# The first block's adaLN scale on TensorE, with the v weights' loads cut and reordered

## The chip, the cores and the metric

The kernel runs on one core of a Trainium2 chip. The metric is the device time of one execution in microseconds (us); lower is better. Before the change the median of three runs is 1084.25 us (1083.64 to 1084.68).

The core has five engines that run side by side, each with its own list of instructions taken in order: TensorE (PE in the profile; its weight loads are listed as PEld), VectorE (DVE), ScalarE (ACT), GpSimd (POOL) and SyncE (SP). Here SyncE only issues DMAs; GpSimd issues some as well. SBUF and PSUM have 128 partitions; TensorE writes its results to PSUM.

## The reference, cut to what matters

Two layers, each of a token mixer and a SwiGLU network, on x of 512 tokens by 1024 channels in float32. Every sub-layer normalizes its input and then shifts and scales it by vectors that come from a conditioning vector c (adaLN). The part that the change touches is the very first one:

```python
def ada_modulation(c, w, b):
    m = jax.nn.silu(c) @ w + b
    shift, scale, gate = jnp.split(m, 3, axis=-1)
    return shift[:, None, :], scale[:, None, :], gate[:, None, :]

shift, scale, gate = ada_modulation(c, mix_ada_w[0], mix_ada_b[0])
h = rms_norm(x, mix_pre_g[0]) * (1.0 + scale) + shift
qkv = (h @ w_qkv).reshape(B, S, 3, SB_HEADS, SB_HEAD_DIM)
```

After it come stick-breaking attention, its output projection, the network, a token-mixing layer and a second network. They are not touched.

## The kernel before, in words

Matrix products are made from float32 operands that are split in two: a high part, which ScalarE rounds to the matmul's format, and a low part, the difference, which VectorE makes. Three products of high and low parts (high by high, high by low, low by high) are added up in PSUM. The 1024 channels are eight blocks of 128, called k = 0 to 7, with the channels of a block on the partitions.

**The start** (lines 324 to 347). SP's queue issues, in this order: `pack` (c, the identity, the pre-norm's gain), the four token tiles of x, the adaLN weights `ra[0]` of block 0, the first and second v weights (`raw`: 256 rows by 512 columns each, the first for the left half of v's columns and the second for the right), `ra[1]`, `ra[2]`, the third v weights (`rawv`), `ra[3]`, the fourth v weights (`rawv`). Each adaLN block is one tile of 128 partitions by 2 by 1026: for each channel of the block (on the partition) the 1024 weights of its scale, then its bias and a one, and the same for its shift. The remaining blocks `ra[4]` to `ra[7]`, and the v weights from the fifth on, are issued later, when a buffer comes free (four for `ra`, two for `raw`).

**Normalizing and turning.** ScalarE takes silu(c) as `sc`, and TensorE spreads it over all partitions with eight matmuls (line 736). The sums of squares of the four token tiles are taken on VectorE (one) and ScalarE (three); `norm0` scales a tile by its reciprocal root on VectorE, and `turn0(tt, q)` turns four of its eight blocks on TensorE into a PSUM bank. `turned0(tt, q, act)` copies such a bank to `xhT` in two pieces of 128 by 256 on ScalarE. `idle0` issues transposes whose results nobody reads.

**The adaLN sums.** `ada_row(k, i)` (line 710) multiplies a block's 1026 numbers by the spread silu(c) on VectorE and adds them up along the row in the same instruction; i = 0 gives 1 + scale, i = 1 the shift. For k = 0, ScalarE then multiplies the scale by the gain (line 787).

**The first step, k = 0** (lines 767 to 807). ScalarE rounds the first row block of the first v weights (`first_high`), makes the high part of block 0's h (`hTh`) in two halves of 256 tokens, and VectorE makes the low part of the weights (`first_low`), h itself in place, and its low part (`low0`). TensorE begins the v products, with four banks per half of v's columns.

**The loop over k = 1 to 7** (line 814). Per k TensorE has 24 matmuls: two halves of the columns, four token tiles, three products. On VectorE stand the two `ada_row` sums of block k + 1 with the low part of block k between them; on ScalarE the high part of block k + 1 (`high0`). The weights of the next two blocks are rounded in the odd steps, and loads are issued there too: `ra[4]` to `ra[7]` in steps 1 to 4, and one or two later v weights.

From line 344 to line 838 the order on TensorE, VectorE and ScalarE is the order in which the code is written (`pe["chain"]`, `dve.chain`, `act.chain`): each instruction is put behind the one before it on its engine. GpSimd and SP have no such chain; the framework places their instructions. PSUM has six banks that are handed round under the tag `b` and two under the tag `p`; a new use of a bank waits for the last reader of the old one.

The v products are followed by those of q and k (`pqk` in the profile), which are mixed with the attention.

Of the kernel before, what the change touches and what calls it, by code (L numbers as in the profile page):

```python
# [8 lines left out]
F32 = mybir.dt.float32  # L9
F32R = mybir.dt.float32r  # L10
AF = mybir.ActivationFunctionType
ALU = mybir.AluOpType

P = 128
T = 512
NT = T // P
D = 1024
KD = D // P
# [7 lines left out]
def trunk(ctx: ExitStack, tc: tile.TileContext, A: dict, out: bass.AP):  # L26
    nc = tc.nc

    consts = ctx.enter_context(tc.tile_pool(name="consts", bufs=1))
    wraw = ctx.enter_context(tc.tile_pool(name="wraw", bufs=2))  # L30
# [3 lines left out]
    small = ctx.enter_context(tc.tile_pool(name="small", bufs=4))  # L34
# [9 lines left out]
    def nm(s):  # L44
        uid[0] += 1
        return f"{s}_{uid[0]}"
# [5 lines left out]
    def bank(name, tag="b"):  # L52
        return psum.tile([P, 512], F32, tag=tag, bufs=6 if tag == "b" else 2, name=nm(name))
# [22 lines left out]
    dve, act = Written(nc.vector), Written(nc.scalar)  # L76
# [22 lines left out]
    def transpose(o, i):  # L99
        last_tp[0] = nc.tensor.transpose(o, i, ident)  # L100
        pe_op(last_tp[0])
# [6 lines left out]
    def load(dst, src, queue=nc.sync):  # L108
        return queue.dma_start(out=dst, in_=src)
# [8 lines left out]
    stream = []  # L118
# [5 lines left out]
    raws = []  # L124

    def wload():

        src, a, b, key = stream[len(raws)]
        if src is None:
            raws.append(block_loads(key[1]))  # L130
            return
        raw = wraw.tile([P, a, b], F32, tag="raw", name=nm("raw"))
        b = load(raw[:], src)
        if key == ("wout", 1):
            ready[2] = b
        raws.append(raw)
# [31 lines left out]
    def block_loads(idx):  # L168

        x = wraw.tile([P, KD, P], F32, tag="raw", name=nm("rawx"))
        y = fwork["raw"].tile([P, KD, P], F32, tag="raw2", name=nm("rawy"))
        load(x[:], A["wx"][idx])
        b = load(y[:], A["wy"][idx])
        if idx == (1, 0):
            order(b, ready[2])
        return x, y
# [138 lines left out]
    def ada0_raw(k):  # L318

        raw = stp.tile([P, 2, D + 2], F32, tag="ra", bufs=4, name=nm("ada0"))  # L320
        load(raw[:], A["ada0w"][k])
        return raw

    pack = consts.tile([P, KD + P + 2 * KD], F32, name="pack")
# [2 lines left out]
    cols = pack[:, KD + P :].rearrange("p (a b) -> p a b", a=2)  # L327
    x0 = [slot(F32, "x0", 1, 1024)[:, 0, :] for _ in range(NT)]
    for tt, xt in enumerate(x0):
        load(xt, A["x"][tt * P : (tt + 1) * P, :])  # L330
    ra = {0: ada0_raw(0)}
    wload()
    wload()
    ra[1] = ada0_raw(1)
    ra[2] = ada0_raw(2)
    for n in (2, 3):
        raws.append(stp.tile([P, 2, 512], F32, name=f"rawv{n}"))
        load(raws[n][:], stream[n][0])
        if n == 2:
            ra[3] = ada0_raw(3)  # L340
    ones_r = consts.tile([P, P], F32R, name="ones")[:]
    scr = stp.tile([P, D + 2], F32, name="scr")
    nc.gpsimd.memset(scr[:, D:], 1.0)
# [3 lines left out]
    sc = consts.tile([P, KD], F32, name="sc")  # L347
# [115 lines left out]
    def hTk(hT, k, lo, n):  # L463
        h, l = hT[k // 2]
        return h[:, k % 2, lo : lo + n], l[:, k % 2, lo : lo + n]
# [198 lines left out]
    def norm0(tt, sd, r1):  # L664
        dve.reciprocal(r1[:], sd[:])
        dve.tensor_scalar(x0[tt], x0[tt], r1[:, 0:1], None, ALU.mult)
# [3 lines left out]
    def turn0(tt, q):  # L670
        ps = bank("tp0", "p" if q and tt > 1 else "b")
        for k in range(4):
            kk = q * 4 + k
            transpose(ps[:, k * P : (k + 1) * P], x0[tt][:, kk * P : (kk + 1) * P])
        tps[tt, q] = ps

    def turned0(tt, q, engine):
        ps = tps[tt, q]
        for k2 in range(2):
            dst = xhT[q * 2 + k2][:, :, tt * P : (tt + 1) * P]  # L680
            src = ps[:, k2 * 256 : (k2 + 1) * 256].rearrange("p (a b) -> p a b", a=2)
            if engine is dve:
                dve.tensor_copy(dst, src)
            else:
                act.activation(dst, src, AF.Copy)
# [24 lines left out]
    def ada_row(k, i):  # L710

        if i == 0:
            ab[k] = small.tile([P, 2], F32, tag="ab", name=nm("ab"))
        w = ra[k][:, i, :]
        dve.scalar_tensor_tensor(
            w, w, 1.0, scr[:], ALU.mult, ALU.mult, accum_out=ab[k][:, i : i + 1]
        )
        if i == 1 and k:
            dve.tensor_scalar(ab[k][:, 0:1], ab[k][:, 0:1], cols[:, 0, k : k + 1], None, ALU.mult)

    ab = {}
# [20 lines left out]
    def idle0(n, into=warm):  # L742
        for i in range(n):
            transpose(into[:, i % 4 * P : (i % 4 + 1) * P], ident)
# [15 lines left out]
        turn0(tt, 1)  # L760
    norm0(2, *r0[2])
    turn0(2, 0)
    turn0(2, 1)
    norm0(3, *r0[3])
    turn0(3, 0)
    turn0(3, 1)
    vb = [[bank("v0") for _ in range(2)], [bank("v1")]]
    idle0(20, vb[0][0])
    ada_row(0, 0)
    ada_row(0, 1)  # L770
    ws = [wtile(2, 512, WIDE) for _ in range(2)]
    got.extend(ws)
# [2 lines left out]
    def first_high(hf, k):  # L775
        act.activation(ws[hf][0][:, k, :], raws[hf][:, k, :], AF.Copy)

    def first_low(hf, k):
        h, l = [t[:, k, :] for t in ws[hf]]
        dve.tensor_tensor(l, raws[hf][:, k, :], h.bitcast(F32), ALU.subtract)  # L780

    for tt in range(NT):
        if tt == NT - 1:
            turned0(0, 1, act)
        turned0(tt, 0, act)
    scale, shift = [ab[0][:, i : i + 1] for i in range(2)]
    act.activation(scale, scale, AF.Copy, scale=cols[:, 0, 0:1])
    first_high(0, 0)
    x00, (h00, l00) = xhT[0][:, 0, :], hTk(hT, 0, 0, T)
    for c in (slice(0, 256), slice(256, T)):  # L790
        act.activation(h00[:, c], x00[:, c], AF.Identity, scale=scale, bias=shift)
    first_low(0, 0)
    dve.tensor_scalar(x00, x00, scale, shift, ALU.mult, ALU.add)
    first_high(1, 0)
    for tt in (2, 3, 1):
        turned0(tt, 1, act)
    vb[1] += [bank("v1", "p") for _ in range(2)] + [bank("v1")]
    vb[0] += [bank("v0") for _ in range(2)]
# [800 lines left out]
def _layout(i):  # L1599

    f = np.ascontiguousarray

    def fout(w):
        m = w.shape[1] // P
        return w.reshape(KD, P, m, P).transpose(2, 1, 0, 3)

    def blocks(a, b):

        return (
            np.concatenate([a[:, :, :4], b[:, :, 4:]], 2),  # L1610
            np.concatenate([a[:, :, 4:], b[:, :, :4]], 2),
        )

    def slabs(w):
        return w.reshape(-1, P, 1, w.shape[1])

    def vhalf(w):

        return w.reshape(4, 2, P, 2, 512).transpose(3, 0, 2, 1, 4)

    a = {}

    a["x"] = i["x"][0][::-1]
    wqkv = i["sb_w_qkv"][0]
    a["wqk"] = np.stack([fout(wqkv[:, :D]), fout(wqkv[:, D : 2 * D])], 1)
    a["wv"] = vhalf(wqkv[:, 2 * D :])
    a["wo"] = slabs(i["sb_w_o"][0])
    gu = [(fout(i["ffn_w_gate"][l]), fout(i["ffn_w_up"][l])) for l in range(2)]
    a["wgu"] = np.stack([np.stack([g[:3], u[:3]], 1) for g, u in gu])
    a["wx"], a["wy"] = [np.stack(t) for t in zip(*[blocks(g[3:], u[3:]) for g, u in gu])]  # L1630
    a["wdown"] = np.stack([slabs(i["ffn_w_down"][l]) for l in range(2)])
    a["win_u"] = fout(i["tm_w_in"][0][:, :D])
    a["win_v"] = vhalf(i["tm_w_in"][0][:, D:])
    a["wout"] = slabs(i["tm_w_out"][0])
    a["ws"] = i["tm_w_s"][0][:, ::-1, ::-1].transpose(2, 0, 1)
    a["bs"] = i["tm_b_s"][0][:, ::-1].reshape(1, D)
    ada, adab = [], []
    for l in range(2):
        for n in ("mix", "ffn"):
            w, b = i[n + "_ada_w"][l], i[n + "_ada_b"][l]  # L1640
            ada.append(w.reshape(KD, P, 3, D).transpose(2, 0, 1, 3))
            adab.append(b.reshape(3, 1, D))
    a["ada"], a["adab"] = np.stack(ada), np.stack(adab)
    w = i["mix_ada_w"][0].reshape(KD, P, 3, KD, P)
    b0 = i["mix_ada_b"][0]
    t = np.zeros((KD, P, 2, D + 2), np.float32)
    for n in range(2):
        part = w[:, :, 1 - n].reshape(D, KD, P)
        t[:, :, n, :D] = part.transpose(1, 2, 0)
        t[:, :, n, D] = b0[(1 - n) * D : (2 - n) * D].reshape(KD, P)  # L1650
    t[:, :, 0, D + 1] = 1.0
    a["ada0w"] = t
    a["pre_g"] = np.stack([i["mix_pre_g"][0], i["ffn_pre_g"][0], i["mix_pre_g"][1], i["ffn_pre_g"][1]])
    a["post_g"] = np.stack(
        [i["mix_post_g"][0], i["ffn_post_g"][0], i["mix_post_g"][1], i["ffn_post_g"][1]]
    )
    r = np.arange(P)
    one = np.ones((P, P), np.float32)
    cols = [
        i["mix_pre_g"][0].reshape(KD, P).T, i["tm_ln_g"][0].reshape(KD, P).T,  # L1660
    ]
    a["pack"] = np.concatenate([i["c"][0].reshape(KD, P).T, np.eye(P, dtype=np.float32), *cols], 1)
    a["consts"] = np.stack([np.where(r[:, None] >= r[None, :], one, 0 * one), one], 1)
    return {k: f(v) for k, v in a.items()}
# [17 lines left out]
```

## Time and profile before

| what | value |
|---|---|
| median of three runs | 1084.25 us |
| the profiled execution | 1085.17 us |
| its span, first to last instruction | 1083.4 us |
| TensorE's mean granted clock | 0.998 |
| TensorE, VectorE, ScalarE, GpSimd busy | 1070.5, 906.5, 592.1, 40.4 us |
| bytes moved by DMA, mean rate | 176.09 MB, 163 GB/s |

How to read it. Times in the rows of a timeline are microseconds from the span's start, then the duration; a row such as `L92 MATMUL v<-wh,hTh ... x4` merges four neighbours of one kind, and its duration reaches from the first one's start to the last one's end. In `out<-in` stand the names of tiles: `ada` and `ra` are the adaLN blocks (the loads are named `ada`), `raw` and `rawv` the v weights as loaded, `wh` and `wl` their high and low parts, `hTh` and `hTl` those of h, `tp` and `xhT` the turned input, `ab` the scale and shift, `sc` silu(c). Brackets at the end of a row give the engine's idle time just before and what ended it. A matmul's end is modelled, and neighbours overlap, so one that is listed with 0.39 us may follow the one before it after 0.23. Line 66 is the helper through which all of VectorE's and ScalarE's instructions of the listing go, line 92 that of the matmuls, line 100 that of the transposes and line 109 that of the loads.

### The profile page before, as it was taken

The numbers are of one execution on the slowest core, as the hardware profiler recorded it, in microseconds if no ns is written. First come the engines' busy times: TensorE is split into PE (matmuls) and PEld (weight loads), VectorE is DVE, ScalarE is ACT, GpSimd is POOL, SyncE is SP. The second block draws the span as 40 slices with busy tenths as digits, with TensorE's granted clock in tenths as the row PEclk, the third lists the DMA queues.
The fourth block names the chain that finished last, engine by engine and source line by source line (L and its number), as shares of the span: only waits on it lengthen the run. The fifth ranks groups of instructions, "written<-read, shape, count | busy, mean of one in ns | idle before, by whom it ended". The sixth has DMA issues, their size and how long they took to land.

```text
span 1083.4 us, 18162 instructions
## 1 busy us (share of the span) xinstructions
PE 1070.5 (99%) x7348; PEld 974.2 (90%) x7348; DVE 906.5 (84%) x1159; ACT 592.1 (55%) x976; POOL 40.4 (4%) x71
## 2 busy tenths in 40 slices
PE   8999999999999999999999999999999999999997
PEld 7888878779999999988887988988999999989896
DVE  6859889759999999987678865759999999879986
ACT  7656767747555555562144535537555555565552
POOL 1021111000000000010000000001000000000000
PEclk9999999999999999999999999999999999999999
DMA  9686454453244454358884585333245443223433
GB/s 363 231 253 176 142 150 156 156 195 137 79 122 171 137 156 136 101 183 286 272 269 174 196 271 173 101 135 126 90 137 175 134 142 129 85 78 99 134 101 154
DMA packets 51154, 176.09 MB, mean 163 GB/s; under 512 B 5627, under 2 KB 6139, under 8 KB 50046
## 3 DMA queue, kind: packets, MB, share of 16 engines
q1 hardware_dynamic: 45022, 153.95, 43.1%
q0 software_dynamic: 6048, 20.98, 6.0%
q8 instruction: 57, 0.93, 0.3%
q14 instruction: 27, 0.22, 0.1%
HBM read 164.43 MB, written 8.39 MB: 160 GB/s over the span
## 4 chain that ended last, share of the span: by engine, by line
PE 83%; DMA 8%; DVE 5%; ACT 2%; issue 1%; SPq 0%; DVEq 0%; ACTq 0%
PE r L92 31%; PE y L92 9%; PE pqk L92 8%; PE X L92 8%; PE v L92 7%; PE gu L92 6%; DMA rawada<-in_ada 4%; PE u L92 4%; PE M L92 3%; PE z L92 2%; DMA rawv<-in_wv 2%; PE av L92 1%; PE tw L100 1%; DMA raw<-in_wdown 1%; DVE wl L66 1%
## 5 line engine op out<-in xcount | busy, mean ns | idle before, releaser
L66 ACT ACTIVATE wh<-raw 128x1024 fp32r<-128x1024 f32 (+1 forms) x112 | 116.6, 1047 | 133.2 <-DMA raw<-in_wdown 52.2
L66 DVE TENSOR_TENSOR wl<-raw,wh 128x1024 fp32r<-128x1024 f32 (+1 forms) x112 | 133.7, 1201 | 51.8 <-ACT wh L66 51.2
L92 PE MATMUL r<-Sh,wh 128*128 128x256 f32 x608 | 167.9, 276 | 0.3 <-ACT e L66 0.3
L92 PE MATMUL r<-Sh,wl 128*128 128x256 f32 x608 | 167.9, 276 | 0.0
L92 PE MATMUL r<-Sl,wh 128*128 128x256 f32 x608 | 167.8, 276 | 0.0
L92 PE MATMUL y<-wh,as 128*128 128x512 f32 x480 | 150.7, 391 | 1.0 <-DVE G L66 1.0
L66 ACT ACTIVATE e<-r 128x256 f32<-128x256 f32 x114 | 43.0, 378 | 133.2 <-PE r L92 133.1
L92 PEld LDWEIGHTS r<-Sh,wh 128*128 128x128 f32 x608 | 114.1, 188 | 0.6 <-ACT e L66 0.5
L92 PEld LDWEIGHTS r<-Sl,wh 128*128 128x128 f32 x608 | 114.1, 188 | 0.1
L92 PEld LDWEIGHTS r<-Sh,wl 128*128 128x128 f32 x608 | 114.1, 188 | 0.0
L92 PEld LDWEIGHTS y<-wh,as 128*128 128x128 f32 x480 | 90.1, 188 | 20.1 <-DVE G L66 1.7
L92 PE MATMUL y<-wl,as 128*128 128x512 f32 x240 | 93.7, 390 | 0.0
L66 DVE TENSOR_TENSOR wl<-f,wh 128x1024 fp32r<-128x1024 f32 x76 | 92.6, 1219 | 0.0
L92 PE MATMUL r<-hTh,wh 128*128 128x256 f32 x304 | 84.0, 276 | 0.0
L92 PE MATMUL r<-hTh,wl 128*128 128x256 f32 x304 | 83.9, 276 | 0.0
L92 PE MATMUL r<-hTl,wh 128*128 128x256 f32 x304 | 83.9, 276 | 0.0
L66 ACT ACTIVATE wh<-f 128x1024 fp32r<-128x1024 f32 x76 | 80.5, 1059 | 5.9 <-DVE f L66 4.7
L92 PE MATMUL X<-wh,as 128*128 128x512 f32 (+1 forms) x240 | 64.8, 346 | 0.0
L92 PE MATMUL r<-hTh,b 128*128 128x256 f32 x304 | 57.9, 276 | 0.0
L92 PEld LDWEIGHTS r<-hTh,wh 128*128 128x128 f32 x304 | 57.1, 188 | 0.4 <-DVE gu L66 0.2
L92 PEld LDWEIGHTS r<-hTl,wh 128*128 128x128 f32 x304 | 57.1, 188 | 0.0
L92 PEld LDWEIGHTS r<-hTh,wl 128*128 128x128 f32 x304 | 57.1, 188 | 0.0
(236 smaller groups left out, 2826.7 us busy)
## 6 DMA issues: line engine op xcount, KB each, us to landing
rawada<-in_ada SPq DMA_DIRECT2D x56, 512.0 KB, 5.0
raw<-in_wdown SPq DMA_DIRECT2D x44, 512.0 KB, 4.4
rawy<-in_wy SPq DMA_DIRECT2D x38, 512.0 KB, 3.6
rawx<-in_wx SPq DMA_DIRECT2D x38, 512.0 KB, 4.0
rawada<-in_ada POOLq DMA_DIRECT2D x24, 512.0 KB, 4.1
ada<-in_ada0w SPq DMA_DIRECT2D x8, 1026.0 KB, 11.2
raw<-in_wqk SPq DMA_DIRECT2D x16, 512.0 KB, 4.0
raw<-in_wgu SPq DMA_DIRECT2D x12, 512.0 KB, 3.6
```

The costliest lines, as they stand in the source:

```text
L66: b = f(*a, **k)
L92: b = nc.tensor.matmul(o, l, r, start=start, stop=stop, skip_group_check=True)
L100: last_tp[0] = nc.tensor.transpose(o, i, ident)
```

## The change

- **Layout.** For block 0 the scale's weights are stored with the summed index on the partitions: partition p holds, for each of the eight blocks of c, the 128 weights that go from channel p of that block of c to the 128 channels of block 0. Bias and one stay where they were.
- **The sum.** Instead of `ada_row(0, 0)` on VectorE, eight TensorE matmuls of plain float32, with those weights as the loaded operand and one column of silu(c) as the moving one, add up the 128 scales in one PSUM column (`sps`). They stand between the first turn of token tile 2 and that of tile 3. The second turn of tile 2 now follows the first of tile 3. GpSimd makes `base` = (bias + 1) times the gain, and ScalarE makes the scale as gain times sum plus `base`.
- **Idle transposes.** 20 become 2.
- **ScalarE and VectorE at k = 0.** Seven pieces are copied ahead of the scale instead of ten; the last piece of tile 3 follows the high part of h, and the first tile's second half joins the other three later. The first half of the high part of h moves to VectorE.
- **Loads.** `ra[0]` comes in two loads, scale and shift. The first and second v weights come in halves of 128 rows: the first halves of both, `ra[1]`, the second halves, `ra[2]`; then the third and the fourth v weights, then `ra[3]`.

```diff
     def ada0_raw(k):
 
         raw = stp.tile([P, 2, D + 2], F32, tag="ra", bufs=4, name=nm("ada0"))
-        load(raw[:], A["ada0w"][k])
+        for c in (slice(0, 1), slice(1, 2)) if k == 0 else (slice(0, 2),):
+            load(raw[:, c, :], A["ada0w"][k][:, c, :])
         return raw
...
     ra = {0: ada0_raw(0)}
-    wload()
-    wload()
-    ra[1] = ada0_raw(1)
-    ra[2] = ada0_raw(2)
+    raws.extend(wraw.tile([P, 2, 512], F32, tag="raw", name=nm("raw")) for _ in range(2))
+    for k in range(2):
+        for n in range(2):
+            load(raws[n][:, k, :], stream[n][0][:, k, :])
+        ra[k + 1] = ada0_raw(k + 1)
     for n in (2, 3):
         raws.append(stp.tile([P, 2, 512], F32, name=f"rawv{n}"))
         load(raws[n][:], stream[n][0])
-        if n == 2:
-            ra[3] = ada0_raw(3)
+    ra[3] = ada0_raw(3)
...
-    def turned0(tt, q, engine):
+    def turned0(tt, q, engine, k2s=range(2)):
         ps = tps[tt, q]
-        for k2 in range(2):
+        for k2 in k2s:
...
     norm0(2, *r0[2])
     turn0(2, 0)
-    turn0(2, 1)
+    ab[0] = small.tile([P, 2], F32, tag="ab", name=nm("ab"))
+    scale, shift = [ab[0][:, i : i + 1] for i in range(2)]
+    base = small.tile([P, 1], F32, name="base")
+    nc.gpsimd.tensor_scalar(
+        base[:], ra[0][:, 0, D : D + 1], ra[0][:, 0, D + 1 : D + 2], cols[:, 0, 0:1], ALU.add, ALU.mult
+    )
+    sps = bank("scale", "p")[:, 0:1]
+    for k in range(KD):
+        mm(sps, ra[0][:, 0, k * P : (k + 1) * P], sc[:, k : k + 1], k == 0, k == KD - 1)
     norm0(3, *r0[3])
     turn0(3, 0)
+    turn0(2, 1)
     turn0(3, 1)
     vb = [[bank("v0") for _ in range(2)], [bank("v1")]]
-    idle0(20, vb[0][0])
-    ada_row(0, 0)
+    idle0(2, vb[0][0])
     ada_row(0, 1)
...
     for tt in range(NT):
-        if tt == NT - 1:
-            turned0(0, 1, act)
-        turned0(tt, 0, act)
-    scale, shift = [ab[0][:, i : i + 1] for i in range(2)]
-    act.activation(scale, scale, AF.Copy, scale=cols[:, 0, 0:1])
+        turned0(tt, 0, act, range(2 - (tt == NT - 1)))
+    act.activation(scale, sps, AF.Identity, scale=cols[:, 0, 0:1], bias=base[:])
     first_high(0, 0)
     x00, (h00, l00) = xhT[0][:, 0, :], hTk(hT, 0, 0, T)
-    for c in (slice(0, 256), slice(256, T)):
-        act.activation(h00[:, c], x00[:, c], AF.Identity, scale=scale, bias=shift)
+    c = [slice(0, 256), slice(256, T)]
+    dve.tensor_scalar(h00[:, c[0]], x00[:, c[0]], scale, shift, ALU.mult, ALU.add)
+    act.activation(h00[:, c[1]], x00[:, c[1]], AF.Identity, scale=scale, bias=shift)
+    turned0(NT - 1, 0, act, (1,))
     first_low(0, 0)
     dve.tensor_scalar(x00, x00, scale, shift, ALU.mult, ALU.add)
     first_high(1, 0)
-    for tt in (2, 3, 1):
+    for tt in (0, 2, 3, 1):
         turned0(tt, 1, act)
...
         part = w[:, :, 1 - n].reshape(D, KD, P)
         t[:, :, n, :D] = part.transpose(1, 2, 0)
+        if n == 0:
+            t[0, :, n, :D] = part[:, 0].reshape(KD, P, P).transpose(1, 0, 2).reshape(P, D)
         t[:, :, n, D] = b0[(1 - n) * D : (2 - n) * D].reshape(KD, P)
```

## The prediction, made before the result was known

> **What bounds the kernel now.** I read the page first, then the waits of the first 80 us, then the chain that ended last in the same stretch. The page:
>
> ```profile
> span 1083.4 us, 18162 instructions
> ...
> PE 1070.5 (99%) x7348; PEld 974.2 (90%) x7348; DVE 906.5 (84%) x1159; ACT 592.1 (55%) x976; POOL 40.4 (4%) x71
> ```
>
> TensorE is busy in all but 13 us. So an edit near the start is worth exactly what it moves the point from which TensorE never stops again. Where it stops today is in the waits of 0 to 80 us (who waited for what: total, times, longest):
>
> ```profile
> ACT wh L66 <- DMA rawv<-in_wv: 3.3, 1, 3.3
> ...
> ACT wh L66 <- DMA raw<-in_wv: 2.5, 2, 2.0
> ...
> PE v L92 <- ACT hTh L66: 1.1, 1, 1.1
> ```
>
> and the chain says what is behind the 1.1 us (start, length, what):
>
> ```profile
> 9.39 16.51 DMA rawv<-in_wv
> ...
> 25.92 1.06 ACT wh L66
> 26.98 0.71 ACT hTh L66
> ...
> 27.73 32.94 PE v L92 x144
> 60.67 14.28 PE pqk L92 x63
> ```
>
> The fourth v weights land at 25.9; ScalarE, whose order is written out, rounds them before it makes hTh of the third block (k = 2), and TensorE waits for that until 27.73. From there it runs without a gap: 144 matmuls in 32.94 us are 5.49 us for one step of 24. Whatever the change does, the time after is the time before minus what the starts of k = 2, k = 3, k = 4 and so on gain, the smallest gain deciding. The next rows are the timeline of ScalarE, TensorE and the queue at those starts:
>
> ```profile
> 20.85 0.50 PE L92 MATMUL v<-wh,hTh 128*128 128x512 f32 x1
> ...
> 23.96 0.21 DVE L66 TENSOR_SCALAR ab<-ab,pack 128x1 f32<-128x1 f32 x1
> ...
> 24.45 12.00 SPq L109 DMA_DIRECT2D raw<-in_wv  x2
> ...
> 31.30 0.82 ACT L66 ACTIVATE hTh<-xhT,ab 128x512 fp32r<-128x512 f32 x1 [2.77 <-DVE ab L66]
> ...
> 35.94 1.06 ACT L66 ACTIVATE wh<-raw 128x1024 fp32r<-128x1024 f32 x1 [2.02 <-DMA raw<-in_wv]
> 36.91 0.80 ACT L66 ACTIVATE hTh<-xhT,ab 128x512 fp32r<-128x512 f32 x1
> ...
> 38.75 0.39 PE L92 MATMUL v<-wh,hTh 128*128 128x512 f32 x1
> ```
>
> The important one is at 35.94. The sixth v weights (second half of the columns, third pair) were issued at 24.45 and land at 35.94, and hTh of k = 4 stands behind their rounding: it ends at 37.71, and TensorE begins k = 4 at 38.75. So only 1.0 us lies between this second late transfer and TensorE. It costs nothing today because the 1.1 us stall came before it.
>
> **The path to the first v matmul.** The start, in order of time:
>
> ```profile
> 3.06 3.49 PEld L92 LDWEIGHTS sc<-pack,sc 128*128 128x128 f32 x16 [3.06 <-ACT sc L66]
> ...
> 3.08 0.51 SPq L109 DMA_DIRECT2D ada<-in_ada0w  x1
> ...
> 6.42 1.30 PEld L100 LDWEIGHTS warm<-pack 128*128 128x128 f32 x6
> ...
> 10.00 1.51 POOL L396 MEMSET G<- 128x1024 f32 x1
> 10.74 0.86 PEld L100 LDWEIGHTS tp<-pack,x 128*128 128x128 f32 x8 [0.60 <-issue]
> ...
> 10.91 2.83 ACT L66 ACTIVATE xhT<-tp 128x256 f32<-128x256 f32 x10
> ...
> 11.24 0.83 DVE L66 TENSOR_SCALAR x<-x,r 128x1024 f32<-128x1024 f32 x1
> 11.83 0.62 POOL L109 DMA_DIRECT2D G<-in_adab  x1 [0.32 <-POOL G L396]
> 11.99 1.22 DVE L66 SCALAR_TENSOR_TENSOR ada<-ada,scr 128x1026 f32<-128x1026 f32 x1
> ...
> 13.01 2.21 PEld L100 LDWEIGHTS v<-pack 128*128 128x128 f32 x20
> ...
> 13.13 1.22 DVE L66 SCALAR_TENSOR_TENSOR ada<-ada,scr 128x1026 f32<-128x1026 f32 x1
> 13.55 0.37 ACT L66 ACTIVATE ab<-ab,pack 128x1 f32<-128x1 f32 x1
> 13.73 0.71 ACT L66 ACTIVATE wh<-raw 128x512 fp32r<-128x512 f32 x1
> ...
> 14.46 1.09 ACT L66 ACTIVATE hTh<-xhT,ab 128x256 fp32r<-128x256 f32 x2
> 14.47 0.69 DVE L66 TENSOR_TENSOR wl<-raw,wh 128x512 fp32r<-128x512 f32 x1
> ...
> 15.22 1.18 PE L92 MATMUL v<-wh,hTh 128*128 128x512 f32 x4
> ...
> 15.59 0.55 DVE L66 TENSOR_SCALAR xhT<-xhT,ab 128x512 f32<-128x512 f32 x1 [0.42 <-ACT hTh L66]
> ```
>
> Two chains meet at 14.46: ScalarE's ten copies out of PSUM from 10.91, and VectorE's two sums of 1.22 us from 11.99. The change takes three copies (0.28 us each) and one sum off that path, but adds a step on TensorE, which sat in its 20 idle transposes.
>
> *The sum by TensorE.* A matmul of plain f32 is two loads and two multiplications in this trace (16 for the eight of sc), so eight matmuls are 16. Three rows price one: 0.218 us (3.49 / 16) at the start, 0.217 (1.30 / 6) in the warm-up transposes, 0.108 (0.86 / 8) for the transposes just before the new step's place. The moving operand is one column here, so I take the load alone at the nearest row's rate: 16 x 0.108 = 1.73 us. The lower bound is one load per matmul, 0.86; the upper is 3.49. Their weights must be there:
>
> ```profile
> ada<-in_ada0w SPq DMA_DIRECT2D x1, 1026.0 KB, 8.8
> ...
> 6.00:8.00 2.00, 2.00 (x11) 2.00 (x11) 1.18 (x5) 1.83 (x5) 0.00 (x0) 1.00 1.00 397
> ...
> 30.00:32.00 2.00, 2.00 (x11) 1.65 (x10) 2.00 (x4) 0.70 (x1) 0.00 (x0) 1.00 1.03 435
> ...
> 34.00:36.00 2.00, 2.00 (x10) 1.68 (x9) 2.00 (x4) 0.06 (x1) 0.00 (x0) 1.00 0.09 35
> ```
>
> (The last columns of the windows are granted clock, DMA share and GB/s.) The whole block, issued at 3.08, lands at 11.9; its first half, 513 KB at 397 GB/s, 1.3 us sooner, at 10.6. The four transposes ahead of the sum load from 10.74 to 11.17, so nothing waits. The sum takes 11.17 to 12.90; the four transposes of the last token tile, which now stand behind it on TensorE, to 13.33; ScalarE, done with its six other copies by 12.6, copies one piece until about 13.75, makes the scale by 13.95 (0.18 from its start to the next row's), and rounds the weights until 14.65. VectorE has the shift at 13.2 with one sum fewer, does half of hTh meanwhile, then the low part of the weights (0.69), and starts on xhT at 15.3, not 15.59. First v matmul: 14.75 for 15.22.
>
> *What is moved beside it.* The second copy of the last tile now follows hTh and is needed by the fourth v matmul; at 0.28 us it comes about 0.2 us late for it, and is repaid while TensorE would wait for VectorE at k = 1 (it began at 20.85, behind VectorE's two sums). The scale's PSUM buffer is handed on to the last transposes, which therefore wait for the scale at 13.95; they and two idle transposes are 6 x 0.108 = 0.65 us and end by 14.6, before the rounding does. GpSimd's small base step has no row; its neighbours, the memset at 10.00 and the issue that ends at 12.45, are the most it can stand behind, and the scale wants it at 13.75. I cost it at nothing, up to 1.3 us of cover.
>
> So the chain on VectorE that leads to hTh of k = 1 is 0.3 us sooner: k = 1 starts at 20.55. The first row of a step after a wait is 0.11 us longer (0.50 against 0.39), so k = 2 is due at 20.55 + 0.11 + 5.49 = 26.15, k = 3 at 31.64, k = 4 at 37.13.
>
> *The transfers.* The pieces of a load become smaller: one adaLN block from 8.2 KB per partition to 4.1, two v weights from 4 KB to 2. The window of 6 to 8 us, in which x moves in 4 KB pieces, shows 397 GB/s at full share, that of 30 to 32, with adaLN blocks in 8.2 KB pieces, 435 / 1.03 = 422, so halving costs 6%: 0.16 us on a block of 2.6 us, and by the same ratio 0.17 on the two weights. All that follows in the queue lands 0.33 us later for the same bytes ahead of it. The fourth weights have one block fewer ahead: 25.9 - 2.6 + 0.3 = 23.6; rounded by 24.7, hTh of k = 2 (ready from 23.96 + 0.21) ends at 25.5, before 26.15. That stall goes. The fourth adaLN block lands where those weights did, 26.2; today hTh of k = 3 begins 4.3 us after the rounding ends at 26.98, so it would begin near 29.3 and end at 30.1, before 31.64. No new stall there.
>
> *What is late next.* The sixth weights. SP's queue carries the same bytes up to them, from the same start, so they land at 35.94 + 0.33 = 36.27. From there to the end of hTh are 0.97 + 0.80: 38.04. TensorE, due at 37.13, waits for it and starts (0.05 behind it, and with the longer first step of 0.11) as if at 38.20. Against 38.75 that is a gain of 0.55 us of the 1.62 that TensorE was ahead. Later steps have more room: the first q weights' low part,
>
> ```profile
> 57.23 1.23 DVE L66 TENSOR_TENSOR wl<-raw,wh 128x1024 fp32r<-128x1024 f32 x1 [2.32 <-ACT wh L66]
> ```
>
> ends at 58.46 for a use at 60.67, and it depends on transfers and VectorE, not on TensorE. The 0.55 reaches the end. The profiled execution took 1085.17 us, 1.8 more than its span and 0.9 more than the median of the three runs; by it the kernel after would show a span of 1082.85, and by the median 1084.25 - 0.55 = 1083.7.
>
> **Rivals.** *The sixth weights come sooner than their bytes say.* From 34 to 36 us the queue moves 35 GB/s: some engines' remainders. Should the new pieces even these out, the landing falls by up to 2 us, the wait at k = 4 goes, and all 1.62 us stay: 1082.6. Against it: no piece after the fourth adaLN block changes.
>
> *TensorE's clock falls.* Eighteen idle transposes go, and while ScalarE and VectorE work from 12.9 to 14.7, TensorE has ten transposes and some idle time. If it fell back to the rate of its start (0.217 per load for 0.108) for as long as that lasted there, from 3.06 to at least 7.72, half of 4.7 us would be lost: k = 4 due at 37.13 + 2.33 = 39.46, 0.7 slower, 1085.0. It decides from a loss of 1.6 us on. For it speaks that transposes were all that ran before 15.22; against it that the first four v matmuls, after seven microseconds of nothing but transposes, took 1.18 us together, which is the full rate, and that the changed kernel runs real matmuls at 11.2. (The granted clock can't decide it: the window of 6 to 8 us shows 1.00 although the loads in it are 0.217 apart.) The Trainium skill (TensorE: Matmul & The Clock Gate, Part 4: PE-mode transpose) says that transposes do not count as work for the clock; by that rule the v matmuls of the kernel before would have begun at half rate, and the trace disagrees with it.
>
> *The eight small matmuls are slow.* Each adds to the same PSUM column. If each waited for the last, the mean duration of the start's rows would count, not their spacing:
>
> ```profile
> L92 PE MATMUL sc<-pack,sc 128*128 128x128 f32 x16 | 3.8, 431 | 3.1 <-ACT sc L66 3.1
> ```
>
> 16 x 0.431 = 6.9 us is 5.2 more than I took; k = 4 is due at 42.3, 3.5 slower, 1087.8. At 3.49 for all it is due at 38.9: no change. It decides above 3.4 us, and shows beyond 0.2% above 5.5. For it speaks that the eight at the start write to different columns, so that no row shows such a chain of one column; against it the q matmuls of the chain, 24 in a row into one bank, which are 0.227 apart (14.28 / 63) while one v matmul of the same size lasts 0.39 (the row at 38.75).
>
> *The stall at k = 2 stays*, because the fourth adaLN block or VectorE takes the weights' place: then only the 0.3 us of the start are left, at most, 1084.0 to 1084.3.
>
> **How the numbers follow.** Forecast 0.60; sixth weights sooner 0.15; clock 0.08; slow small matmuls 0.10; stall stays 0.07. The bounds of the small sum alone do not move the forecast: at 0.86 us TensorE only waits longer at k = 4, at 2.8 it is just in time. The range takes the forecast, the sixth weights sooner, the stall, and the milder half of the rest: 1082.5 to 1085.1. What a measurement of this kernel can tell from no change is about 0.2%, 2.2 us. Faster by that needs the sixth weights sooner and a small sum at its lower bound: 0.04. Slower by that needs the slow sum above 5.5 us, or a disturbed order later: 0.06. Within it: 0.90.
>
> **What would show it.** Right: eight matmuls into the scale in about 1.7 us from 11.2; first v matmul near 14.75; no idle time ahead of k = 2; a new idle stretch of about 0.8 us ahead of k = 4, behind hTh, behind a rounding that waits for the sixth weights near 36.3; TensorE's unbroken run from 38.1. Wrong: those weights landing before 35.4 or after 36.8, a sum over 3.4 us, TensorE's loads spaced by 0.2 us after 12, or any wait at k = 2 or k = 3.

## The result: 10.8 us slower, by matmuls that the change does not touch

The changed kernel takes 1094.74 us (median of five runs, 1094.38 to 1095.26) against 1083.97 (1083.64 to 1084.68): a ratio of 1.010, 95% interval 1.0085 to 1.0114. The forecast was 1083.7, the range 1082.5 to 1085.1. The profiled execution took 1095.22 us.

The page after, with two of the costliest groups (the last columns: busy us, mean ns of one, idle time before):

```profile
span 1093.4 us, 18171 instructions
...
PE 1082.9 (99%) x7346; PEld 979.8 (90%) x7346; DVE 906.2 (83%) x1158; ACT 592.1 (54%) x975; POOL 40.2 (4%) x72
...
L92 PE MATMUL r<-Sh,wl 128*128 128x256 f32 x608 | 167.9, 276 | 0.0
L92 PE MATMUL y<-wh,as 128*128 128x512 f32 x480 | 152.5, 395 | 0.0
```

The same two groups on the page before:

```profile
L92 PE MATMUL r<-Sh,wl 128*128 128x256 f32 x608 | 167.9, 276 | 0.0
...
L92 PE MATMUL y<-wh,as 128*128 128x512 f32 x480 | 150.7, 391 | 1.0 <-DVE G L66 1.0
```

TensorE is still busy in 99% of the span; it does not wait more, it is slower, and only in some of its work: the y matmuls (the projections back to x) take 395 ns for 391, the r matmuls 276 as before. The chain that ended last shows it better, because its rows are unbroken runs (start, length, count). After:

```profile
16.50 44.81 PE v L92 x192
61.30 14.63 PE pqk L92 x63
...
224.42 20.93 PE y L92 x90
...
292.72 167.28 PE r L92 x1476
...
615.28 16.86 PE u L92 x144
...
695.48 6.65 PE sv L92 x60
```

and before, where the first run of 63 is the 14.28 us that the prediction shows:

```profile
222.57 20.48 PE y L92 x90
...
290.29 167.29 PE r L92 x1476
...
611.33 16.34 PE u L92 x144
...
689.62 6.65 PE sv L92 x60
```

Divide length by count. The q and k matmuls are 0.2322 us apart after and 0.2267 before, the y ones 0.2326 and 0.2276. The r matmuls (256 columns) are 0.1133 in both, the sv ones 0.1108. So in these runs matmuls of 512 columns have lost 0.005 to 0.0055 us each, hundreds of microseconds after the edited code has ended. Some of 256 columns have lost too: the u matmuls are 0.1171 apart after and 0.1135 before. The groups of 512 columns in which one operand is a weight are v 384, pqk 384, y 912 and X 270, 1950 in all. At 0.0055 us each they would make up 10.7 us, nearly the whole result, but that agreement is chance: not all of them lose it, and the sums under `a2_noshift` put about a third of the loss on matmuls of 256 columns. At the end of the v products the difference was still only 61.30 - 60.67 = 0.63.

The start went partly as forecast. Its rows after (PEld: weight loads):

```profile
11.43 1.86 PEld L92 LDWEIGHTS scale<-sc,ada 128*128 128x128 f32 x16
...
13.13 1.56 PEld L100 LDWEIGHTS tp<-pack,x 128*128 128x128 f32 x8
...
14.28 0.38 ACT L66 ACTIVATE xhT<-tp 128x256 f32<-128x256 f32 x1 [1.33 <-PE tp L100]
...
16.15 1.46 PE L92 MATMUL v<-wh,hTh 128*128 128x512 f32 x4
```

The sum took 1.86 us, 1.73 was forecast. But the eight transposes behind it load 0.195 apart, not 0.108, ScalarE waits 1.33 us for them, and the first v matmul comes at 16.15, not 14.75. The windows say why (granted clock, DMA share and GB/s are the last three):

```profile
12.00:14.00 2.00, 2.00 (x17) 2.00 (x17) 1.79 (x3) 0.94 (x4) 0.75 (x2) 0.84 0.95 374
14.00:16.00 2.00, 2.00 (x11) 1.74 (x10) 0.96 (x2) 1.73 (x5) 0.00 (x0) 0.50 0.96 391
16.00:18.00 2.00, 2.00 (x10) 1.69 (x9) 1.97 (x5) 2.00 (x8) 0.00 (x0) 0.80 1.09 440
```

The clock was at half for about 3.4 us: the three windows of 2 us lack 0.32, 1.0 and 0.4 us of full clock, and at half rate a loss lasts twice as long. This is not where the 10.8 us went: two of the five runs had a mean granted clock of 1.000, and they took 1094.38 and 1094.63 us. (The clock's records begin at 6.54 us in this trace and at 8.14 in that of the kernel before, with a rise to full; ahead of its first record the view gives 1.00. So the 1.00 that the prediction reads between 6 and 8 us was not measured.) Later on ScalarE:

```profile
24.04 1.06 ACT L66 ACTIVATE wh<-rawv 128x1024 fp32r<-128x1024 f32 x1 [1.03 <-DMA rawv<-in_wv]
...
36.63 1.06 ACT L66 ACTIVATE wh<-raw 128x1024 fp32r<-128x1024 f32 x1 [4.10 <-DMA raw<-in_wv]
```

The fourth v weights land at 24.04 (forecast 23.6) and no stall is left ahead of k = 2 (the chain's 192 v matmuls from 16.50 are one run); the sixth land at 36.63 (forecast 36.27).

### The profile page after: what moved, and what is told of

Same layout as the page of the kernel before. It is cut to its first block, busy times and chain, and to the rows that moved or that the text cites. A ratio compares the mean times of both kernels' runs of the same rounds, so it can differ in the third digit from the quotient of the medians.

```text
span 1093.4 us, 18171 instructions
## 1 busy us (share of the span) xinstructions
PE 1082.9 (99%) x7346; PEld 979.8 (90%) x7346; DVE 906.2 (83%) x1158; ACT 592.1 (54%) x975; POOL 40.2 (4%) x72
## 4 chain that ended last, share of the span: by engine, by line
PE 93%; DVE 3%; issue 2%; DMA 1%; ACT 1%; POOL 0%; DVEq 0%; SPq 0%; ACTq 0%; POOLq 0%
PE r L92 32%; PE y L92 19%; PE v L92 8%; PE X L92 8%; PE pqk L92 6%; PE gu L92 6%; PE u L92 4%; PE M L92 3%; PE tp L100 1%; PE z L92 1%; PE tw L100 1%; PE av L92 1%; PE sv L92 1%; PE adaps L92 1%; DVE ga L66 1%
```

## The experiments

**The theory.** The edited code adds one new name, `base`, to the pool of small tiles. The pool gives it four buffers of 32 bytes per partition, and the pools that come later (the activations, `s4`, among them) start 128 bytes higher: 67,776 instead of 67,648 in the built programs. The split weights (`wh`, `wl`) lie in an earlier pool and stay at 10,528. The kernel is written for a fixed distance between the two: `placed` shifts each weight tile to a chosen place in a line of 64 numbers (256 bytes) and adds a literal 8. The weights' pool begins 32 bytes into its line, and the literal brings the wide weights to 64 bytes, which is where `s4` begins in its line in the kernel before. (A sixth weight buffer, which the later parts add behind `s4`, moves with the activations.) The theory, P below, is that moving one operand of a matmul half a line against the other costs the 0.005 to 0.0055 us a matmul. Its main rival, S, is that something at the changed start leaves TensorE slower.

**First set: the move alone, the change without it, the move made good, and a whole line.**

`a1_pad` is the kernel before and one line more:

```diff
     ada_row(0, 0)
+    small.tile([P, 1], F32, name="base")
```

> The kernel before with one more name in the pool of small tiles, never written or read; the pool grows by 128 bytes per partition and all pools behind it move up by as much, as they do in the changed kernel. Theory P (the 10.8 us come from where the tiles lie: matmuls whose two operands come from pools that moved against each other are spaced by 0.232 us instead of 0.227): the time of the changed kernel without its start, 1083.97 + 9.4 to 10.4, about 1094. Rival S (something in the changed start leaves TensorE slower for the rest of the run): 1084.0, no change.

Measured: 1094.94 us against 1083.63, ratio 1.0105 (1.009 to 1.012). Its chain:

```profile
61.17 14.70 PE pqk L92 x63
...
224.26 20.93 PE y L92 x90
...
292.85 167.28 PE r L92 x1476
...
695.55 6.65 PE sv L92 x60
```

A tile that nobody writes or reads costs 11.3 us, and the unbroken runs are about as long as those of the changed kernel, although the start is that of the kernel before. S does not explain this.

`a2_noshift` is the changed kernel with `base` in a buffer of an old name:

```diff
-    base = small.tile([P, 1], F32, name="base")
+    base = small.tile([P, 1], F32, tag="sx", name="base")
```

> The changed kernel with the new base value in a buffer of an old name, so that nothing moves. Theory P: matmuls at 0.227 again, and what is left is the start alone; hTh of k = 4 ended at 38.40 in the changed kernel, so k = 4 starts as if at 38.56 against 38.75 before: 1083.8, within 0.3 us of the kernel before. Rival S: 1094.7 as with the whole change.

Measured: 1082.97 against 1083.63, ratio 0.9998 (0.9989 to 1.0008). The rest of the change is worth 0.7 us by the medians and 0.2 by the ratio, which the interval can't tell from nothing; 1083.8 was expected. With the changed start and no move the loss is gone, so S has fallen.

Against this run the changed kernel shows what the move costs each kind. Added up over the two traces, from the start of each matmul to that of the next, it takes longer by 3.5 us in y, 1.3 in X of 512 columns, 1.1 in q and k, and by 4.0 us in matmuls of 256 columns: u 1.4, gu 1.2, X 0.8, M 0.6. In v it is 0.8 us, but there the fall of the clock and the wait at k = 4, which the changed kernel lacks, are mixed in. The sv matmuls are as they were.

TensorE's and ScalarE's timelines and the chain:

```profile
38.14 0.50 PE L92 MATMUL v<-wh,hTh 128*128 128x512 f32 x1 [0.83 <-ACT hTh L66]
```

```profile
36.33 1.06 ACT L66 ACTIVATE wh<-raw 128x1024 fp32r<-128x1024 f32 x1 [4.29 <-DMA raw<-in_wv]
37.29 0.80 ACT L66 ACTIVATE hTh<-xhT,ab 128x512 fp32r<-128x512 f32 x1
```

```profile
60.20 14.28 PE pqk L92 x63
```

Here the prediction can be read off: the sixth weights at 36.33, hTh behind them, TensorE idle for 0.83 us ahead of k = 4 (forecast: 0.8), and the v products over at 60.20, 0.47 sooner than before (forecast: 0.55). The last number is weak: in other profiles of kernels that load as the kernel before does and have nothing moved by part of a line, the v products end anywhere from 59.81 (`c3_noidle`) to 60.78 (`c2_128col`).

`a3_moved` is the changed kernel with the weights moved inside their buffers by the same 32 numbers:

```diff
-        pool, first = (wpools[0][0], 8) if turn[0] < wpools[0][1] else (wpools[1][0], 0)
+        pool, first = (wpools[0][0], 40) if turn[0] < wpools[0][1] else (wpools[1][0], 0)
```

> The changed kernel, with the split weights' places inside their buffers moved by the same 128 bytes (32 numbers) as the pools behind. Theory P in its form that only the place of one operand relative to the other within a 256-byte line counts: 1083.8. Theory P in another form (the absolute address of the later pools counts): 1094.7. Rival S: 1094.7.

Measured: 1083.91 against 1083.63, ratio 1.0001 (0.9992 to 1.001). The activations lie where they lie in the changed kernel, and the loss is gone: it is the distance between the operands that counts, not the address of one.

```profile
60.58 14.28 PE pqk L92 x63
...
222.21 20.46 PE y L92 x90
```

`a4_pad2` is the kernel before with two such unused names, 256 bytes.

> The kernel before with two unused names in the pool of small tiles, 256 bytes: everything behind moves by one whole line. Theory P with lines of 256 bytes: 1084.0, no change. If any move of the later pools costs, or more move costs more: 1094 or above. Rival S: 1084.0.

Measured: 1083.87 against 1083.63, ratio 1.0002 (0.9993 to 1.0012). A whole line costs nothing.

**Two more distances.** `b4_pad64` and `c4_pad192` give the unused name two and six buffers:

```diff
+    small.tile([P, 1], F32, name="base", bufs=2)
```

> The kernel before with an unused name of two buffers in the pool of small tiles: everything behind moves by 64 bytes, a quarter of a line. If the distance of the two operands within the line sets the cost step by step, the time lies between 1083.6 and 1094.9; if any distance but the one of the kernel before costs the same, 1094.9; if only half a line costs, 1083.6.

> The kernel before with an unused name of six buffers in the pool of small tiles: everything behind moves by 192 bytes, three quarters of a line. If the cost is even in the distance (the same 64 bytes forward and back), about 1111.5; if each kind of matmul has its own good distance, another time between 1083.5 and 1112; only a whole line costs nothing in either case.

Measured: 1111.54 against 1083.50 (ratio 1.0257, 1.0243 to 1.0271) and 1105.33 against 1083.67 (1.0199, 1.0184 to 1.0214). The first lies outside all three times that were expected; the second is the case in which each kind has its own good distance. At 64 and at 192 bytes:

```profile
62.17 14.44 PE pqk L92 x63
...
224.71 20.99 PE y L92 x90
294.23 174.46 PE r L92 x1476
...
704.96 6.65 PE sv L92 x60
```

```profile
60.55 14.70 PE pqk L92 x63
...
223.66 20.80 PE y L92 x90
...
292.83 172.93 PE r L92 x1476
...
699.83 6.65 PE sv L92 x60
```

Now the r matmuls pay too: 0.1182 and 0.1172 apart, for 0.1133. Half a line spares the r matmuls, and a quarter either way does not. The code places their weights a quarter of a line off the wide ones (`NARROW` 16, `WIDE` 0), but it places those of u there too, and u pays at half a line; so what makes the good distances of a kind is not shown. The sv matmuls, whose two operands lie in one pool and move together, are at 0.1108 in every case. The cost is neither even nor steadily growing in the distance; of the four places tried only the kernel's own is good for all kinds.

**Second set: what eats the gain at the start.** All three have nothing moved in memory. `b1_sixth` is `a2_noshift` with the sixth v weights issued ahead of the seventh adaLN block:

```diff
-        for j in {1: (4,), 2: (5,), 3: (6,), 4: (7,)}.get(k, ()):
+        for j in {1: (4,), 2: (5,), 4: (7,)}.get(k, ()):
...
-            ws = [wget(("wv", hf, k // 2 + 1), 0) for hf in range(2)]
+            ws = []
+            for hf in range(2):
+                ws.append(wget(("wv", hf, k // 2 + 1), 0))
+                if k == 3 and hf == 0:
+                    ra[6] = ada0_raw(6)
```

> The changed kernel with nothing moved in memory, and with the sixth v weights issued ahead of the seventh adaLN block instead of behind it. Theory L (what eats most of the gain at the start is the landing of the sixth v weights): they land about 2.5 us sooner, the idle 0.83 us of TensorE ahead of k = 4 goes, and k = 4 starts where TensorE is due, about 37.2: 1.1 us less than without this, 1081.9. Rival (something else stands right behind them, the sums on VectorE or the seventh adaLN block): at most 0.3 us less, 1082.7.

Measured: 1082.51 against 1083.50, ratio 0.9989 (0.998 to 0.9998), 0.6 us above the forecast and nearer to the rival's 1082.7. By the trace the theory holds, in this one execution: the weights land at 34.15 and TensorE runs through k = 4, as expected,

```profile
15.77 44.88 PE v L92 x192
60.65 14.28 PE pqk L92 x63
```

but the run of v takes 44.88 us, and its windows show half clock again:

```profile
14.00:16.00 2.00, 1.72 (x12) 1.39 (x11) 1.28 (x3) 2.00 (x6) 0.00 (x0) 0.78 0.97 396
16.00:18.00 2.00, 2.00 (x6) 1.61 (x5) 1.97 (x4) 2.00 (x8) 0.00 (x0) 0.50 1.08 435
18.00:20.00 2.00, 2.00 (x9) 1.58 (x9) 2.00 (x6) 1.61 (x5) 0.00 (x0) 0.87 0.99 410
```

With the sixth weights out of the way nothing downstream absorbs that loss any more.

`b2_wide` adds 127 columns to the small matmuls:

```diff
-    sps = bank("scale", "p")[:, 0:1]
+    sps = bank("scale", "p")[:, 0:P]
...
-        mm(sps, ra[0][:, 0, k * P : (k + 1) * P], sc[:, k : k + 1], k == 0, k == KD - 1)
+        mm(sps, ra[0][:, 0, k * P : (k + 1) * P], sc[:, k : k + 1].to_broadcast([P, P]), k == 0, k == KD - 1)
...
-    act.activation(scale, sps, AF.Identity, scale=cols[:, 0, 0:1], bias=base[:])
+    act.activation(scale, sps[:, 0:1], AF.Identity, scale=cols[:, 0, 0:1], bias=base[:])
```

> As b1_sixth, with silu(c) spread over 128 columns in the eight small matmuls, so that they stream 128 columns instead of one. Theory C (one-column matmuls count as too little work for the clock, which therefore falls to half for 3.4 us in some executions): the sum takes as long as before (its 16 loads set the pace), the granted clock stays at 1.00 from 10 to 18 us, and no run is 0.7 us or more above the others: 1081.9 with a narrow spread. Rival (the clock falls because of the waiting around the scale, or the sum is paced by its columns): dips as before, or the sum grows from 1.8 us to over 3 and the time by about 1 us.

Measured: 1082.39 against 1083.50, ratio 0.9991 (0.9982 to 1.0). The sum takes 1.95 us with 128 times the columns, so its 16 loads do set the pace. The clock is at 1.00 in the windows from 14 to 18 us, and the v products take

```profile
16.44 43.81 PE v L92 x192
60.26 14.28 PE pqk L92 x63
```

1.07 us less than in `b1_sixth`, though they begin 0.67 later, because the first tile of x landed later in this execution (6.07 against 5.18). The runs spread from 1081.6 to 1084.57, so the narrow spread that was expected is not there, and the two kernels can't be told apart by their times.

`b3_loads` is the kernel before with two of the loads' moves and nothing of the sum; the loads are not cut. The fourth v weights go ahead of the fourth adaLN block, as in the change:

```diff
     for n in (2, 3):
         raws.append(stp.tile([P, 2, 512], F32, name=f"rawv{n}"))
         load(raws[n][:], stream[n][0])
-        if n == 2:
-            ra[3] = ada0_raw(3)
+    ra[3] = ada0_raw(3)
```

and the sixth ahead of the seventh block, as in `b1_sixth`.

> The kernel before with the loads alone reordered: the third and fourth v weights ahead of the fourth adaLN block, the sixth ahead of the seventh block; the scale still summed on VectorE, the 20 idle transposes kept. Theory L: the stall ahead of k = 2 (1.1 us) goes and none follows at k = 4; k = 4 is due at 20.85 + 0.11 + 3 x 5.45 = 37.3, not 38.75: 1.4 us less than the kernel before, 1082.2. Rival (the gain at the start comes from TensorE's sum): no change, 1083.6.

Measured: 1082.06 against 1083.50, ratio 0.9988 (0.9979 to 0.9997): near the forecast 1082.2, and the fastest median of all. TensorE runs without a gap from k = 1:

```profile
21.23 38.38 PE v L92 x168
59.61 14.28 PE pqk L92 x63
```

59.61 is 1.06 sooner than before and sooner than with the sum on TensorE (60.26, 60.65), but these are single profiles, and that of `c3_noidle`, with the loads of the kernel before, has 59.81. It is the medians, 1.44 us apart with an interval clear of 1, that show the gain. The order of the loads carries the gain; the new sum adds none that these runs can show.

**Third set: what makes the clock fall.** Each is the kernel before with another filling for the 2 us ahead of the first v matmul: narrow f32 matmuls, the same with 128 columns, and nothing.

```diff
-    idle0(20, vb[0][0])
+    for _ in range(10):
+        mm(vb[0][0][:, 0:1], ident, sc[:, 0:1], True, True)
```

> The kernel before with its 20 idle transposes replaced by 10 unread f32 matmuls of one column (20 loads, the same 2.2 us of TensorE). Theory C (a load with one column to stream counts as too little work for the clock): the granted clock falls to 0.50 for 3.4 us somewhere between 12 and 19 us in the profile, and in a good part of the runs; the median rises by 0.3 to 1.0 us and the spread widens upwards. Rival (waiting, not the narrow matmuls): clock at 1.00 throughout, 1083.5.

`c2_128col` has `vb[0][0][:, 0:P]` and `sc[:, 0:1].to_broadcast([P, P])` there.

> As c1_onecol with 128 columns each, so that only the number of columns differs. Theory C: clock at 1.00 throughout, 1083.5, as with the transposes. If it falls here too, the columns are not what counts.

```diff
-    idle0(20, vb[0][0])
+    idle0(2, vb[0][0])
```

> The kernel before with 2 idle transposes for 20 and nothing else changed: TensorE waits about 2 us ahead of the first v matmul. Theory C: two microseconds of waiting are too short, clock at 1.00, 1083.5. Rival (waiting makes the clock fall): 0.50 for 3.4 us, the median up by 0.3 to 1.0 us.

Measured, against 1083.67: 1084.09 (ratio 1.0001, 0.9992 to 1.001), 1083.87 (1.0003, 0.9994 to 1.0013), 1083.28 (0.9996, 0.9986 to 1.0005). No difference, and the granted clock is 1.00 at the start of all three profiles. TensorE's row of `c1_onecol`, then that of `c3_noidle`:

```profile
13.26 2.29 PE L92 MATMUL v<-sc,pack 128*128 128x1 f32 x20
```

```profile
15.74 1.23 PE L92 MATMUL v<-wh,hTh 128*128 128x512 f32 x4 [1.61 <-ACT hTh L66]
```

Neither 2.3 us of one-column matmuls nor 1.6 us of waiting brought the clock down by itself. In the first 30 us it fell in three of the four profiles with the one-column sum (the changed kernel, `a3_moved`, `b1_sixth`; not in `a2_noshift`) and in none of the other ten. By the traces' clock records it fell 6.83 us after the rise to full in all three, for 3.41 us. In the 3.41 us before the fall TensorE loaded 11 transposes and 16 of the one-column loads in the changed kernel. The same stretch of `c1_onecol`, 3.41 to 6.83 us after its rise, holds the same 11 and 16, and its clock stayed up. So the narrow matmuls do not decide it alone, and my theory of them is not shown; what exactly makes the clock fall stays open, with one profile for each kernel.

## Why the prediction was wrong

- **The step that failed** is the one on GpSimd's small base step: "I cost it at nothing, up to 1.3 us of cover." Its time is indeed hidden (0.33 us from 10.88 on in the profile after), but I priced only its time and not its tile. The tile moves every later pool by 128 bytes against the split weights, and by `a1_pad` that alone is the whole loss (11.3 us by the medians there, 10.8 for the change). No rival named it. So the premise that "an edit near the start is worth exactly what it moves the point from which TensorE never stops again" failed: the sum behind "The 0.55 reaches the end" took TensorE's spacing of 0.227 as given, and in the changed kernel the q and k matmuls were 0.232 apart.
- **The shape of the small gain was right**, as `a2_noshift` shows: the stall at k = 2 gone, a new one of 0.83 us at k = 4 behind the sixth v weights (0.8 forecast). The size is not confirmed: it is -0.66 us by the medians for -0.55, but the interval takes in zero. The stall at k = 2 that the sum starts from, 1.1 us, is also that of one execution; with the same loads it is 0.8 us in the profile of `a4_pad2`, 0.5 in that of `c1_onecol`, 0.6 in that of `c2_128col`, and none in that of `c3_noidle`. `b1_sixth` and `b3_loads` show that the sixth weights were what was late next: issued sooner, they leave no wait at k = 4 in the profiles.
- **Sizes.** The sum by TensorE 1.86 us for 1.73; the sixth weights at 36.63 (36.33 in `a2_noshift`) for 36.27; the first v matmul, without the fall of the clock, at 14.98 for 14.75.
- **The clock rival** had 0.08 and came true in the profiled execution as a mechanism, but not as a price: a fall of 3.4 us delays the first v matmul by about 0.9 us (16.15 against 14.98 in `a2_noshift`, of which 0.24 was there before the sum began: 11.43 against 11.19), and the wait of 0.83 us at k = 4 was there to absorb most of it. The Trainium skill (TensorE: Matmul & The Clock Gate, Part 1) gives half rate and a window of about 3.4 us, and the trace agrees with both. The Trainium skill's rule of thumb on the same page (Part 1, HAM oscillation), no idle gaps of TensorE above about 3.4 us, is not enough here: once at work, TensorE of the changed kernel waited for less than 0.5 us at a time, and the clock fell. `c3_noidle` agrees with the rule: 1.61 us of waiting, and no fall.

## What to carry to other kernels

A new small buffer is not free because it is small: look where it moves the buffers behind it, above all when a kernel places its matmul operands by hand against a literal. When the time changes far from the edit, compare the spacing of unbroken runs of one kind of matmul in both chains before looking for waits, and test with the buffer alone. Where a wait is taken away, read off how far the next late transfer stands behind it; that, not the length of the wait, is the gain.

## What the runs showed of the hardware

The spacing of f32r matmuls depends on how far apart the two operands lie within a line of 256 bytes per partition. For q and k (512 columns) it is 0.2267 us at the kernel's own distance and after a whole line, 0.2292 at 64 bytes off, 0.2333 at 128 and at 192; for r (256 columns) 0.1133 at 0 and 128, 0.1182 at 64, 0.1172 at 192; for u (256 columns too) 0.1135 at 0 and 0.1171 at 128. Moving the other operand by the same 128 bytes restores it (`a3_moved`). What in TensorE's reads causes this the runs don't show.
